# Hybrid decoder trunk on one core: stick weights as scan differences, value products in fours, narrow scores, and broadcast products moved ahead

## The chip, the cores and the metric

The kernel runs on one core of a Trainium2 chip. The metric is the device time of one execution in microseconds; the time before is the median of three runs. The engines are named as in the profile: PE is TensorE (its weight loads, which overlap its products, are PEld), DVE is VectorE, ACT is ScalarE, POOL is GpSimd, SP issues the DMAs. Matrix products write PSUM, which has eight banks here, and POOL works on SBUF alone.

## The reference, cut to what matters

Two layers. Each normalises the input, projects it once, mixes it with two kinds of attention, gates both and projects back.

```python
# A) stick-breaking attention, 4 heads x 64, strictly causal, blocks of 128
z = einsum(q, k) * scale
ls_z = log_sigmoid(z)
log_surv = where(mask, ls_z - z, 0)          # log(1 - sigmoid(z))
acc = (sum of log_surv over the later keys)
a = where(mask, exp(ls_z + acc), 0)          # sigmoid(z_k) * prod over later keys of (1 - sigmoid)
o = einsum(a, v)
# B) dilated sliding window, 12 heads x 64, patterns (128,1), (512,4), (2048,16)
s = where(mask, einsum(q, [k_prev, k_own]) * scale, -inf)
m = max(s); p = exp(s - m); l = sum(p); o = einsum(p, v) / l; log_den = m + log(l)
# over the three patterns
alpha = softmax(log_den); out = sum(alpha * o)
# each branch is gated, then one output projection, then the residual
```

S is 2048, the model width 1024. In pattern 0 as the kernel orders the keys, every block of 128 queries needs one block of 128 keys; in patterns 1 and 2 it needs its own block and the one before, except where the block is the first of its residue class.

## The kernel before, in words

A layer is a projection, the stick stage (`_stick`), the dilated stage (`_dilated`) and the output projection. The order of PE's instructions in both attention stages is held by hand (`pin`); on the other engines the framework orders the instructions.

**Stick stage.** Two head pairs. For each of the 16 blocks of queries, from the last to the first, the keys are taken from the diagonal back in pieces of up to 512: these are the units, 40 a pair, 80 a layer; 16 of a pair's 40 hold the diagonal and have one to four key blocks, the other 24 have four. `front(u)` makes the scores of both heads (lines 541 and 542, two products of the rounded float32 type; line 544 puts the mask on the diagonal). ACT makes `g`, the sigmoid of the negated score (line 549), and `b`, the sigmoid of the score (line 550). DVE's scan (line 551) multiplies `g` up from the last key to the first, and goes on in the next unit from the value that the previous unit left. POOL multiplies `b` by the scan (line 557). `mid(u)` transposes the weights on PE (line 570) and copies them to SBUF (line 572, head 0 on ACT, head 1 on DVE). `back(u)` multiplies them with the values (line 584). The loop issues `front(u + 2)`, `mid(u)`, and after every second unit `back` of the two units before. Buffers: six slices each for the scan, `g`, `b` and the transposed weights, four PSUM banks for scores, three for transposes.

**Dilated stage.** Six head pairs, 48 steps each: 16 blocks in each of the three patterns. `front(g)` makes the scores of both heads, two products per head with 256 key columns (line 732), also where only 128 are used; DVE adds the mask and takes the maximum (line 734), ACT makes the exponentials and their sum (line 738). `mid(g)` transposes (line 753) and copies (line 755, even steps on ACT, odd ones on DVE). Every fourth step `back` multiplies four steps with the values (line 767) and ACT copies the result (lines 772 to 777). Steps run three ahead. While a pair is under way, the statistics of the pair before are made (`stats_a` and `stats_b`, on POOL, PE, ACT and DVE, steps 1 and 5), and its three patterns are weighted: `weigh` broadcasts the weights by a product (line 837) and DVE multiplies (line 838), one call a step from step 15 to 30; `gate`, after every fourth of them, sums the patterns and gates them on POOL (lines 845 to 847). `make_q` orders the queries for patterns 1 and 2 by POOL copies (lines 668 and 672).

Of the kernel before, what the change touches and what calls it, by code (L numbers as in the profile page):

```python
# [13 lines left out]
AF = mybir.ActivationFunctionType  # L14
ALU = mybir.AluOpType
# [444 lines left out]
def _stick(tc, mem, sb_scr, g_scr, mix, ident, ident_r):  # L460
    nc = tc.nc
# [12 lines left out]
    setH = ("H5", "H4", "H3", "H2")  # L474
    wk0 = mem.get("G0", [128, 12, 513])
    wk1 = mem.get("G1", [128, 12, 512])
    r_s = Slices([wk0[:, i] for i in range(6)])
    gam = Slices([wk0[:, 6 + i] for i in range(6)])
    b_s = Slices([wk1[:, i] for i in range(6)])
    at_s = Slices([wk1[:, 6 + i] for i in range(6)])  # L480
    nc.gpsimd.memset(wk0[:, 6:12, 512:513], 1.0)
    qs_, ks1, ks2, vn, gt = {}, {}, {}, {}, {}

    def prep(pr, jq):
# [44 lines left out]
    pin = tc.keep_in_program_order  # L529
    carry, prod, ats, obs = {}, {}, {}, {}  # L530

    def front(u):
        pr, i, lo, hi = units[u]
        n, kq, top = hi - lo, lo // 512, hi == 128 * (i + 1)
        nn = max(n, 256)
        qs = slice(128 * (i % 4), 128 * (i % 4) + 128)
        zs = []
        for h in range(2):
            z = z_r.get([128, 512])
            qt = qs_[pr, i // 4, h][:, qs]  # L540
            pin(nc.tensor.matmul(z[:, :nn], qt, ks1[pr, kq, h][:, :nn], start=True, stop=False))
            pin(nc.tensor.matmul(z[:, :nn], qt, ks2[pr, kq, h][:, :nn], start=False, stop=not top))  # L542
            if top:
                pin(nc.tensor.matmul(z[:, n - 128:n], id_b, tri, start=False, stop=True))
            zs.append(z)
        prod[u] = []
        for h, z in enumerate(zs):
            b, g, r = b_s.get(), gam.get(), r_s.get()
            nc.scalar.activation(g[:, 512 - n:512], z[:, :n], AF.Sigmoid, scale=-0.125)  # L549
            nc.scalar.activation(b[:, :n], z[:, :n], AF.Sigmoid, scale=0.125)  # L550
            nc.vector.tensor_tensor_scan(  # L551
                out=r[:, 0:n + 1][:, ::-1], data0=g[:, 512 - n:513][:, ::-1],
                data1=z[:, 0:1].to_broadcast([128, n + 1]),
                initial=1.0 if top else carry[h][:, 0:1],
                op0=ALU.mult, op1=ALU.bypass)
            carry[h] = r
            nc.gpsimd.tensor_tensor(out=b[:, :n], in0=b[:, :n], in1=r[:, 1:n + 1], op=ALU.mult)  # L557
            prod[u].append(b)
        if pr == 0 and i % 4 == 0 and lo == 0:
            todo.append(prep(1, i // 4))  # L560
            next(todo[-1])

    def mid(u):
        pr, i, lo, hi = units[u]
        n = hi - lo
        ats[u] = []
        for h, b in enumerate(prod.pop(u)):
            ps = t_r.get([128, 512])
            for j in range(n // 128):
                pin(nc.tensor.transpose(ps[:, 128 * j:128 * j + 128], b[:, 128 * j:128 * j + 128], ident))  # L570
            at = at_s.get()
            (nc.vector.tensor_copy if h else nc.scalar.copy)(at[:, :n], ps[:, :n])
            ats[u].append(at)

    def back(u):
# [16 lines left out]
                nc.sync.dma_start(out=mix[0][pr].rearrange("p (c a) -> p c a", c=NT), in_=gt[pr])  # L592

    todo = []
    LEAD, BATCH = 2, 2
    load(1)
    for u in range(LEAD):
        front(u)
# [18 lines left out]
def _dilated(tc, mem, v_scr, qk_scr, g_scr, mix, masks, sel, ident, neg1):  # L617
    nc = tc.nc
    pin = tc.keep_in_program_order
    mk = mem.get("M", [128, 732])  # L620
# [3 lines left out]
    o_r = mem.bank_ring(5)  # L624
    w_r = mem.bank_ring(6, 7)
    pa, pb = mem.get("H0", [128, 2, 2, 256]), mem.get("H1", [128, 2, 2, 256])
    pe_s = Slices([pa[:, 0], pa[:, 1], pb[:, 0], pb[:, 1]])
    ta, tb = mem.get("H6", [128, 2, 2, 2, 128]), mem.get("H7", [128, 1024])
    td = mem.get("H5", [128, 2, 2, 2, 128])
    ts_s = Slices([td[:, 0], td[:, 1], ta[:, 0], ta[:, 1], tb[:, 0:512].rearrange("p (c h q) -> p c h q", c=2, h=2)])  # L630
    xa = mem.get("X", [128, 1024])
# [21 lines left out]
    def load_q(pr):  # L653
        qq[pr] = [[], []]
        for h in range(2):
            t = q_r.get([128, S])
            nc.sync.dma_start(out=t, in_=qk_scr[pr, h])
            qq[pr][h].append(t)
# [33 lines left out]
    for i in range(4):  # L692
        t = gt_r.get([128, 4, 128])
# [5 lines left out]
    def geom(p, b):  # L699
        if p == 0:  # L700
            return b, 0, True
        c, n = (b // 4, b % 4) if p == 1 else (0, b)
        return c, n, n == 0

    def front(g):
        pr, p, b = g // 48, g // 16 % 3, g % 16
        if (p, b) == (0, 0):
            o3s[pr] = mem.get(f"G{pr % 2}", [128, 3, NT, 128])
            sts[pr] = st_r.get([128, 2, 3, 2, NT])
        st = sts[pr]  # L710
        c, n, first = geom(p, b)
        u0 = 0
        if p == 0:
            w0 = min(b, 14) * 128
            u0 = 128 * b - w0
        else:
            run, stp = (32, 4) if p == 1 else (8, 1)
            w0 = 0 if first else run * (n - 1)
        un = 128 if first else 256
        m0 = M_OWN[p] + 128 - un  # L720
        sc = s_r.get([128, 2, 256])
        pe = pe_s.get()
        for h in range(2):
            qb = qq[pr][h][p].bitcast(F32R)[:, 128 * b:128 * b + 128]
            for s in range(2):
                kt = kk[pr][h][s]
                if p == 0:
                    kv = kt[:, w0:w0 + 256]
                else:
                    kv = kt.rearrange("p (c a) -> p c a", c=NT)[  # L730
                        :, c::stp, w0:w0 + 2 * run].rearrange("p c (w a) -> p w c a", w=2)
                pin(nc.tensor.matmul(sc[:, h], qb, kv, start=s == 0, stop=s == 1))  # L732
        for h in range(2):
            nc.vector.tensor_tensor_reduce(  # L734
                out=pe[:, h, :un], in0=sc[:, h, u0:u0 + un], in1=mk[:, m0:m0 + un],
                scale=-0.125, scalar=3.0e38, op0=ALU.add, op1=ALU.min,
                accum_out=st[:, 0, p, h, b:b + 1])
            nc.scalar.activation(pe[:, h, :un], pe[:, h, :un], AF.Exp, scale=-1.0,  # L738
                                 bias=st[:, 0, p, h, b:b + 1], accum_out=st[:, 1, p, h, b:b + 1])
        pes[g] = pe  # L740
# [3 lines left out]
    def mid(g):  # L744
        p, b = g // 16 % 3, g % 16
        first = geom(p, b)[2]
        pe = pes.pop(g)
        tp = t_r.get([128, 2, 2, 128])
        nch = 1 if first else 2
        for ch in range(nch):  # L750
            for h in range(2):
                w = 0 if first else 1 - ch
                pin(nc.tensor.transpose(tp[:, ch, h], pe[:, h, 128 * w:128 * w + 128], ident))  # L753
        ts = ts_s.get()
        (nc.vector.tensor_copy if g % 2 else nc.scalar.copy)(ts[:, :nch], tp[:, :nch])  # L755
        tss[g] = ts

    def back(g0):
# [37 lines left out]
    def stats_b(pr, eng):  # L796
# [3 lines left out]
        for s in range(2):  # L800
            ps = w_r.get([128, 512])
# [4 lines left out]
            for h in range(2):  # L806
                pin(nc.tensor.matmul(ps[:32, 256:384], mk[:, 656 - 16 * h:688 - 16 * h],
                                     x1[:, s, NT * h:NT * h + NT].rearrange("p j a -> p (j a)"),
                                     start=h == 0, stop=h == 1))
            nc.scalar.copy(sm[:, s].rearrange("p q a -> p (q a)"), ps[:32, :384])  # L810
        nm = sm[:, 0]
        ll = sm[:, 1]
        mn = tb[0:32, 896:1024]
        ew = tb[0:32, 512:896].rearrange("p (q a) -> p q a", q=3)
        nc.vector.tensor_tensor(out=mn, in0=nm[:, 0], in1=nm[:, 1], op=ALU.min)
        nc.vector.tensor_tensor(out=mn, in0=mn, in1=nm[:, 2], op=ALU.min)
        eng.tensor_tensor(out=ew, in0=mn.unsqueeze(1).to_broadcast([32, 3, 128]), in1=nm, op=ALU.subtract)
# [12 lines left out]
    def weigh(pr, c):  # L830
        o3 = o3s[pr]
        if c % 4 == 0:
            gts[pr] = gt_r.get([128, 4, 128])
            nc.sync.dma_start(out=gts[pr], in_=g_scr[2 + pr, :, 128 * c:128 * c + 512].rearrange(
                "p (c a) -> p c a", c=4))
        wb = w_r.get([128, 3, 128])
        pin(nc.tensor.matmul(wb, selr[:, c], wr, start=True, stop=True))
        nc.vector.tensor_tensor(out=o3[:, :, c], in0=o3[:, :, c], in1=wb, op=ALU.mult)
# [16 lines left out]
    LEAD = 3  # L855
# [3 lines left out]
    for g in range(total):  # L859
        pr, t = g // 48, g % 48  # L860
        if t % 8 == 2:
            load_v(g // 8 + 1)
        if t == 2:
            make_q(pr, 2)
        if pr + 1 < NPAIR:
            if t == 16:
                load_k(pr + 1)
            if t == 24:
                load_q(pr + 1)
            if t == 36:  # L870
                make_q(pr + 1, 1)
        if g + LEAD < total:
            front(g + LEAD)
        mid(g)
        if g % 4 == 0 and g:
            back(g - 4)
        if pr:
            if t == 1:
                stats_a(pr - 1, nc.gpsimd)
            elif t == 5:  # L880
                stats_b(pr - 1, nc.gpsimd)
            elif 15 <= t < 31:
                weigh(pr - 1, t - 15)
                if t % 4 == 2:
                    gate(pr - 1, (t - 15) // 4)
        yield
    back(total - 4)
    m7 = [mem.get("F5", [128, NT, 128], F32R), mem.get("F6", [128, NT, 128], F32R)]
# [93 lines left out]
```

## Time and profile before

| | |
|---|---|
| time, median of 3 runs | 3229.11 us (3222.7 to 3229.73) |
| profiled execution, its own time | 3228.57 us |
| its span, first to last instruction | 3226.8 us |
| mean granted TensorE clock | 0.993 |
| PE busy | 3137.9 us, 97% of the span |
| DVE busy | 1648.3 us, 51% |
| ACT busy | 1534.4 us, 48% |
| POOL busy | 1234.4 us, 38% |

The busy times are those of the whole span. Matmuls are pipelined and their ends are modelled, so PE's busy time contains short waits. Instructions of ACT and DVE are recorded with their latency: neighbours overlap by some tens of ns, and the distance from start to start is shorter than the duration. The chain of waits is followed back from the last instruction, at each step to what released it; a piece of it is the part of an instruction that the chain uses.

### The profile page before, as it was taken

The page shows a single profiled execution, that of the slowest core. Times are in us where ns is not written, and L with a number is a line of the kernel's source. Part 1 is how long each engine was busy: PE and PEld are TensorE (multiplying, and loading weights), DVE is VectorE, ACT ScalarE, POOL GpSimd, SP SyncE. Part 2 cuts the span into 40 slices and gives each one's busy share as a digit, 9 for nine tenths or more (in the row PEclk, how much of TensorE's full clock was granted, in tenths as well). Part 3 has the DMA queues.
Part 4 walks back from the last instruction along what each step waited for, and adds up shares of the span by engine and source line. Part 5 has one row for each costly group of instructions (what it writes and reads, how often), then busy time and mean ns, then how long its engine had stood idle before and what let it go on. Part 6 is the DMA issues. An engine that isn't in the chain of part 4 may idle for free.

```text
span 3226.8 us, 59494 instructions
## 1 busy us (share of the span) xinstructions
PE 3137.9 (97%) x21968; PEld 2683.2 (83%) x21968; DVE 1648.3 (51%) x4147; ACT 1534.4 (48%) x4317; POOL 1234.4 (38%) x1302
## 2 busy tenths in 40 slices
PE   8999999999999999989999999999999999999899
PEld 8888888887777999878898888888877789988787
DVE  6134440015988777764141444301169887777721
ACT  5123331114878998962031233211158789988510
POOL 1067751102664444451010677511036734444500
PEclk9999999999999999999999999999999999999999
DMA  5123346317023556454442233463160235663443
GB/s 198 63 73 113 112 138 181 122 48 204 15 83 93 165 155 193 117 164 150 128 135 72 70 113 105 149 189 104 59 186 21 83 106 151 178 187 100 140 145 108
DMA packets 324066, 396.40 MB, mean 123 GB/s; under 512 B 20160, under 2 KB 270016, under 8 KB 313536
## 3 DMA queue, kind: packets, MB, share of 16 engines
q1 hardware_dynamic: 323776, 392.60, 40.0%
q8 instruction: 174, 2.85, 0.4%
q14 instruction: 116, 0.95, 0.1%
HBM read 235.24 MB, written 148.90 MB: 119 GB/s over the span
## 4 chain that ended last, share of the span: by engine, by line
PE 81%; DVE 5%; ACT 4%; POOL 4%; issue 3%; DMA 2%; SPq 0%; POOLq 0%; ACTq 0%; DVEq 0%
PE b L310 11%; PE b L311 11%; PE b L309 11%; PE b L732 7%; PE b L767 5%; PE b L753 5%; PE b L451 4%; PE b L453 4%; PE b L452 4%; PE b L935 4%; PE b L936 4%; PE b L932 3%; PE b L584 3%; PE b L367 2%; ACT H L738 2%
## 5 line engine op out<-in xcount | busy, mean ns | idle before, releaser
L738 ACT ACTIVATE H<-H,T 128x256 f32<-128x256 f32 (+1 forms) x1152 | 522.7, 457 | 45.9 <-DVE T L734 43.4
L311 PE MATMUL b<-F,F 128*128 128x512 f32 (+1 forms) x1344 | 484.1, 360 | 0.4 <-DVE F L282 0.3
L734 DVE CUSTOM_DVE_ANT_0 H<-b,M 128x256 f32<-128x256 f32 (+1 forms) x1152 | 368.6, 361 | 168.9 <-PE b L732 66.2
L732 PE MATMUL b<-F,F 128*128 128x256 f32 x2304 | 412.3, 303 | 0.3 <-DVE T L734 0.3
L557 POOL TENSOR_TENSOR G<-G,G 128x512 f32<-128x512 f32 (+3 forms) x320 | 320.5, 1017 | 228.5 <-DVE G L551 171.6
L551 DVE TENSOR_TENSOR_SCAN G<-G,b 128x513 f32<-128x513 f32 (+3 forms) x320 | 336.5, 1085 | 33.0 <-ACT G L550 32.7
L732 PEld LDWEIGHTS b<-F,F 128*128 128x128 f32 x2304 | 326.4, 190 | 20.1 <-issue 19.5
L310 PE MATMUL b<-F,G 128*128 128x512 f32 (+1 forms) x896 | 324.7, 362 | 0.0
L309 PE MATMUL b<-F,G 128*128 128x512 f32 (+1 forms) x896 | 324.3, 362 | 0.0
L310 PE MATMUL b<-F,F 128*128 128x512 f32 (+1 forms) x896 | 323.2, 361 | 0.0
L309 PE MATMUL b<-F,F 128*128 128x512 f32 (+1 forms) x896 | 321.9, 359 | 0.0
L753 PE MATMUL b<-ident,H 128*128 128x128 f32 x1800 | 292.9, 274 | 11.4 <-ACT H L755 5.5
L311 PEld LDWEIGHTS b<-F,F 128*128 128x128 f32 x1344 | 253.7, 189 | 38.4 <-DVE F L282 0.8
L135 POOL TENSOR_SCALAR U<-U 128x16 f32<-128x16 f32 (+1 forms) x80 | 33.7, 421 | 536.1 <-DVE U L334 315.5
L767 PE MATMUL b<-H,H 128*64 128x128 f32 x3600 | 229.8, 277 | 0.8 <-DVE H L755 0.8
L753 PEld LDWEIGHTS b<-ident,H 128*128 128x128 f32 x1800 | 215.6, 141 | 16.5 <-ACT H L755 8.6
L549 ACT ACTIVATE G<-b 128x512 f32<-128x512 f32 (+3 forms) x320 | 179.5, 563 | 103.6 <-PE b L542 87.8
L738 ACT ACTIVATION_READ_ACCUMULATOR H<-H,T 128x1 f32 x1152 | 219.3, 190 | 0.0
L767 PEld LDWEIGHTS b<-H,H 128*64 128x64 f32 x3600 | 193.8, 137 | 25.9 <-issue 23.4
L212 POOL TENSOR_TENSOR F<-H,F 128x1024 fp32r<-128x1024 f32 x22 | 53.9, 2456 | 380.7 <-ACT F L211 164.0
L333 ACT ACTIVATE H<-b 128x512 f32<-128x512 f32 x96 | 57.5, 600 | 294.8 <-PE b L311 293.8
L309 PEld LDWEIGHTS b<-F,G 128*128 128x128 f32 x896 | 168.9, 189 | 26.6
(165 smaller groups left out, 6844.2 us busy)
## 6 DMA issues: line engine op xcount, KB each, us to landing
qk_l<-H SPq DMA_DIRECT2D x192, 256.0 KB
F<-qk_l SPq DMA_DIRECT2D x48, 1024.0 KB
v_l<-S SPq DMA_DIRECT2D x288, 128.0 KB
H<-v_l SPq DMA_DIRECT2D x72, 512.0 KB
F<-qk_l SPq DMA_DIRECT2D x48, 512.0 KB
g_l<-S SPq DMA_DIRECT2D x64, 256.0 KB
G<-mixa_l SPq DMA_DIRECT2D x32, 448.0 KB
H<-in_w_in SPq DMA_DIRECT2D x24, 512.0 KB
```

The lines of the kernel that those rows point to most:

```text
L309: nc.tensor.matmul(ps, hT(q, 0, k)[:, cs], wh, start=k == 0, stop=False)
L310: nc.tensor.matmul(ps, hT(q, 0, k)[:, cs], wl, start=False, stop=False)
L311: nc.tensor.matmul(ps, hT(q, 1, k)[:, cs], wh, start=False, stop=k == NK - 1)
L451: nc.tensor.matmul(ps, wh[:, k, w], hT(tq, 0, k), start=k == 0, stop=False)
L549: nc.scalar.activation(g[:, 512 - n:512], z[:, :n], AF.Sigmoid, scale=-0.125)
L551: nc.vector.tensor_tensor_scan(out=r[:, 0:n + 1][:, ::-1], data0=g[:, 512 - n:513][:, ::-1], data1=z[:, 0:1].to_broadcast([128, n + 1]), i ...
L557: nc.gpsimd.tensor_tensor(out=b[:, :n], in0=b[:, :n], in1=r[:, 1:n + 1], op=ALU.mult)
L732: pin(nc.tensor.matmul(sc[:, h], qb, kv, start=s == 0, stop=s == 1))
L734: nc.vector.tensor_tensor_reduce(out=pe[:, h, :un], in0=sc[:, h, u0:u0 + un], in1=mk[:, m0:m0 + un], scale=-0.125, scalar=3.0e38, op0=ALU. ...
L738: nc.scalar.activation(pe[:, h, :un], pe[:, h, :un], AF.Exp, scale=-1.0, bias=st[:, 0, p, h, b:b + 1], accum_out=st[:, 1, p, h, b:b + 1])
L753: pin(nc.tensor.transpose(tp[:, ch, h], pe[:, h, 128 * w:128 * w + 128], ident))
L767: pin(nc.tensor.matmul(ob[64 * h:64 * h + 64, b % 4], vq[(pr * 3 + p) * 2 + (b - ch) // 8][:, (b - ch) % 8, 64 * h:64 * h + 64], ts[:, ch, h],
```

## The change

In the stick stage a weight is written as the difference of two neighbouring values of the scan, `r[k+1] - r[k]`, in place of sigmoid times scan; the second sigmoid goes, all copies of transposed weights go to ACT, value products are issued for four units at a time, the scan and `g` have four slices, the transposed weights ten. In the dilated stage a step that uses one key block makes scores of 128 columns; the copies of the transposed exponentials go to ACT in one step of four and to DVE in three; the exponentials have a fifth buffer, for which the statistics move to other places; `weigh` and `gate` run from step 17 to 32 and stand between `front` and `mid` of their step.

```diff
-    r_s = Slices([wk0[:, i] for i in range(6)])
-    gam = Slices([wk0[:, 6 + i] for i in range(6)])
+    r_s = Slices([wk0[:, i] for i in range(4)])
+    gam = Slices([wk0[:, 4 + i] for i in range(4)])
     b_s = Slices([wk1[:, i] for i in range(6)])
-    at_s = Slices([wk1[:, 6 + i] for i in range(6)])
-    nc.gpsimd.memset(wk0[:, 6:12, 512:513], 1.0)
+    at_s = Slices([wk1[:, 6 + i] for i in range(6)] + [wk0[:, 8 + i, :512] for i in range(4)])
+    nc.gpsimd.memset(wk0[:, 4:8, 512:513], 1.0)
...
             nc.scalar.activation(g[:, 512 - n:512], z[:, :n], AF.Sigmoid, scale=-0.125)
-            nc.scalar.activation(b[:, :n], z[:, :n], AF.Sigmoid, scale=0.125)
...
-            nc.gpsimd.tensor_tensor(out=b[:, :n], in0=b[:, :n], in1=r[:, 1:n + 1], op=ALU.mult)
+            nc.gpsimd.tensor_tensor(out=b[:, :n], in0=r[:, 1:n + 1], in1=r[:, 0:n], op=ALU.subtract)
...
-            (nc.vector.tensor_copy if h else nc.scalar.copy)(at[:, :n], ps[:, :n])
+            nc.scalar.copy(at[:, :n], ps[:, :n])
...
-    LEAD, BATCH = 2, 2
+    LEAD, BATCH = 2, 4
...
-    pe_s = Slices([pa[:, 0], pa[:, 1], pb[:, 0], pb[:, 1]])
     ta, tb = mem.get("H6", [128, 2, 2, 2, 128]), mem.get("H7", [128, 1024])
+    pe_s = Slices([pa[:, 0], pa[:, 1], pb[:, 0], pb[:, 1], tb[:, 512:1024].rearrange("p (h k) -> p h k", h=2)])
...
-        u0 = 0
-        if p == 0:
-            w0 = min(b, 14) * 128
-            u0 = 128 * b - w0
-        else:
+        un = 128 if first else 256
+        if p:
             run, stp = (32, 4) if p == 1 else (8, 1)
             w0 = 0 if first else run * (n - 1)
-        un = 128 if first else 256
...
-                    kv = kt[:, w0:w0 + 256]
+                    kv = kt[:, 128 * b:128 * b + 128]
...
-                        :, c::stp, w0:w0 + 2 * run].rearrange("p c (w a) -> p w c a", w=2)
-                pin(nc.tensor.matmul(sc[:, h], qb, kv, start=s == 0, stop=s == 1))
+                        :, c::stp, w0:w0 + run * un // 128].rearrange("p c (w a) -> p w c a", a=run)
+                pin(nc.tensor.matmul(sc[:, h, :un], qb, kv, start=s == 0, stop=s == 1))
...
-                out=pe[:, h, :un], in0=sc[:, h, u0:u0 + un], in1=mk[:, m0:m0 + un],
+                out=pe[:, h, :un], in0=sc[:, h, :un], in1=mk[:, m0:m0 + un],
...
-        (nc.vector.tensor_copy if g % 2 else nc.scalar.copy)(ts[:, :nch], tp[:, :nch])
+        (nc.scalar.copy if g % 4 == 1 else nc.vector.tensor_copy)(ts[:, :nch], tp[:, :nch])
...
-        mn = tb[0:32, 896:1024]
-        ew = tb[0:32, 512:896].rearrange("p (q a) -> p q a", q=3)
+        mn = xa[0:32, 768:896]
+        ew = nm
...
             front(g + LEAD)
+        if pr and 17 <= t < 33:
+            weigh(pr - 1, t - 17)
+            if t % 4 == 0:
+                gate(pr - 1, (t - 17) // 4)
         mid(g)
...
-            elif 15 <= t < 31:
-                weigh(pr - 1, t - 15)
-                if t % 4 == 2:
-                    gate(pr - 1, (t - 15) // 4)
```

## Rows read from the trace of the kernel before

**Rows 1.** Busy us by stretch: length, PE, PEld, DVE, ACT, POOL (instructions), clock, DMA.
```profile
765.00:1016.00 251.00, 231.67 (x2115) 186.35 (x2114) 224.76 (x272) 185.00 (x416) 164.75 (x168) 0.98 0.28 80
1016.00:1400.00 384.00, 376.23 (x3866) 345.99 (x3867) 286.06 (x1355) 349.68 (x1336) 163.96 (x209) 1.00 0.54 153
1104.94:1123.07 18.13, 18.13 (x188) 17.11 (x189) 17.16 (x69) 16.04 (x58) 13.65 (x17) 1.00 0.46 139
2365.00:2620.00 255.00, 236.00 (x2141) 189.93 (x2139) 225.88 (x272) 186.17 (x417) 164.73 (x168) 0.98 0.29 84
```

**Rows 2.** Groups by form, 765 to 1016: busy us, mean ns, idle before.
```profile
L551 DVE TENSOR_TENSOR_SCAN G<-G,b 128x513 f32<-128x513 f32 x112 | 138.5, 1263 | 16.5 <-ACT G L550 16.5
L557 POOL TENSOR_TENSOR G<-G,G 128x512 f32<-128x512 f32 x112 | 129.4, 1163 | 106.1 <-DVE G L551 78.8 <-PE b L570 22.4 <-PE b L542 3.0
...
L550 ACT ACTIVATE G<-b 128x512 f32<-128x512 f32 x112 | 70.0, 628 | 0.0
...
L572 DVE COPY G<-b 128x512 f32<-128x512 f32 x56 | 37.5, 670 | 1.9 <-PE b L570 1.6
```

**Rows 3.** Chain of waits, 984 to 1002: start us, us, what.
```profile
984.81 1.90 PE b L584 x32
986.71 0.43 PE b L541
987.14 0.24 PE b L542
...
987.89 0.42 ACT G L550
...
989.33 0.62 ACT G L572
...
990.61 1.90 PE b L584 x32
```

**Rows 4.** Timeline, 990 to 997: start us, us, instruction, idle before and releaser.
```profile
993.20 0.60 ACT L549 ACTIVATE G<-b 128x512 f32<-128x512 f32 x1 [1.77 <-PE b L542]
...
994.32 1.28 DVE L551 TENSOR_TENSOR_SCAN G<-G,b 128x513 f32<-128x513 f32 x1 [0.59 <-ACT G L550]
...
995.75 1.28 POOL L557 TENSOR_TENSOR G<-G,G 128x512 f32<-128x512 f32 x1 [1.20 <-DVE G L551]
```

**Rows 5.** Chain of waits, 1024 to 1036 (pattern 0, first pair).
```profile
1026.33 1.55 ACT H L738 x8
1027.88 0.26 ACT H L755
...
1028.92 0.47 ACT G L772
...
1030.43 1.55 ACT H L738 x8
```

**Rows 6.** Chain of waits, 1146 to 1174 (pattern 0, third pair).
```profile
1151.00 1.02 PE b L767 x16
...
1157.13 1.02 PE b L767 x16
...
1159.05 0.47 PE b L732 x4
...
1160.74 2.29 POOL F L672 x4
...
1166.21 0.44 PE b L837
...
1167.35 1.03 PE b L767 x16
```

**Rows 7.** Groups by form, whole span: DVE copy of a narrow step.
```profile
L755 DVE COPY H<-b 128x256 f32<-128x256 f32 x96 | 40.2, 418 | 0.0
```

**Rows 8.** Pieces of the chain: rounded transposes, and float32 products of 128 columns.
```profile
214.23 1.32 PE b L367 x16
...
1153.39 0.44 PE b L807 x4
```

## The prediction

> **What bounds the kernel now.** I read the views in this order: busy time by stage, the groups of the stick-breaking stage, the chain of waits inside a few of its cycles, and then the chain in the dilated stage. Only these two stages are touched, and the second layer repeats the first.
>
> Busy time by stage [rows 1] shows TensorE (PE) busy for 231.67 of the 251 us of the stick stage, and for 376.23 of the 384 us of the dilated stage. PE therefore nearly sets the pace of both. Time can be won only from its idle remainder, 19.3 us in each stick stage (19.0 in the second layer) and 7.8 us in a dilated stage, or from PE's own work. PE's ends are modelled, so short waits hide in its busy time and the remainder is a lower bound.
>
> In the stick stage VectorE (DVE) is nearly as full, 224.76 us. Its scans take 1263 ns, its copies 670 [rows 2]. The chain over one cycle of two full units [rows 3] runs from one burst of value products at 984.81 to the next at 990.61, that is 5.80 us. The burst takes 1.90, two score products 0.67, then four sigmoids on ScalarE (ACT), one behind the other from 987.4 to 989.3 (one of their pieces is shown), then the ACT copy of 0.62 that the next transposes wait for. The second sigmoid thus stands in the chain, and the scan waits for it too: in the timeline [rows 4] the first sigmoid starts at 993.20, the scan only at 994.32, 0.59 us idle, released by L550. GpSimd (POOL) starts its product 0.15 us after the scan's end.
>
> In the dilated stage, pattern 0 of a layer's first head pair is a chain of ACT alone [rows 5]: 4.10 us for a group of four steps (1026.33 to 1030.43), made of eight exponentials at 0.39 (1.55 for four), two copies of 0.26 and one of 0.47. In later pairs the chain is PE's [rows 6]: per group one burst of 1.02, scores at 0.47 a step and transposes, about 4.0. There the group with the statistics takes 6.13 (1151.00 to 1157.13), and the next two take 10.22 (to 1167.35). Two plain groups and the first broadcast product (0.44) would be 8.5, so 1.7 us are the wait of that product for POOL, whose work in the chain starts with a cast at 1160.74 and lets the product go at 1166.21. Three weighting groups in pattern 1 [rows 1] last 18.13 us, with PE busy without a gap and DVE for 17.16 us.
>
> **The change part by part: the stick stage.** The sum is made against the profiled execution, 3228.57 us (its span is 3226.8); the median of the runs shown is 3229.11, half a microsecond more.
>
> *Second sigmoid out, difference instead of product.* 160 ACT instructions a layer of at most 628 ns [rows 2] go. The POOL instruction stays one subtraction for one product, with the same sizes; I price it the same, 1.16 us, bounds zero either way since no engine or operand size changes. What comes out of the chain is two sigmoids per unit, about 1 us per unit, in a loop that PE closes anyway.
>
> *All copies to ACT.* 80 copies a layer leave DVE (the 56 full ones are 37.5 us [rows 2], the 24 shorter about 0.4 each), and ACT takes them at 0.62 or less [rows 3]. ACT loses 0.63 and gains 0.62 on one of its two heads: it ends with two sigmoids fewer and one copy more per unit. DVE falls from 224.76 by some 47 to 178 us and is no longer beside PE.
>
> *Value products of four units.* The work is the same. Half of the restarts fall away: the first score product after a burst takes 0.43 where the second takes 0.24 [rows 3], so about 0.2 us for 20 bursts a layer, 4 us. But the burst grows to 2 x 1.90 = 3.8 us, and nothing else can be issued on PE behind it. Scores are issued two units ahead, so the scans of two units must cover it. Worked through for four full units: burst 3.8, first scores 0.67, one sigmoid 0.6, two units of scans 4 x 1.26 = 5.0, subtraction 1.2, last transposes 0.4: 11.7 us, against 2 x 5.80 = 11.6 now. Full units win nothing. But 16 of the 40 units of a head pair have one to four blocks at the diagonal, mean 2.5, so a unit has 3.4 blocks in the mean. There the loop shrinks with the blocks to some 10.0 us, while the stage now takes 251 us for 20 such sets, 12.5 each with the start. The ceiling is PE's idle time and the restarts, 19 + 4 = 23 us a layer; the floor of the gain is none. I take 15, two thirds of the ceiling: **-30 us** for both layers.
>
> *Fewer scan and gate buffers (six to four).* A scan must wait for the subtraction two units back instead of three. Two units are four scans of 1.26 us, and the subtraction ends 1.4 us after its scan [rows 4], so it is covered; uncovered it would cost up to 1.2 us per unit where POOL is held up. Nothing.
>
> **The dilated stage.** *128 keys instead of 256.* 21 of the 48 steps of a pair (16 in pattern 0, four in pattern 1, one in pattern 2) with four products each, 12 pairs: 1008 products. Today one takes 0.47 / 4 = 0.119 us [rows 6]. The trace has no such product with 128 columns. Below, the nearest row is the 128-column transposes of the same rounded type, each with its own weights, 1.32 / 16 = 0.082 [rows 8]. Above, it is a plain float32 product of 128 columns, two instructions of 0.44 / 4 = 0.11 each, 0.22 [rows 8]. I take 0.082, because type and weight load are the same. In pattern 0 this frees PE (by 0.6 us per group), and ACT sets the pace. In the other first steps it frees 0.15 us each; of five a pair I count the two that lie outside weighting groups: 0.3 x 12, with the first pairs of the layers -4.5 us.
>
> The Trainium skill, "TensorE: Matmul & The Clock Gate", section "LDWEIGHTS (loading the stationary operand)", prices a load of 128 columns at 107 ns whatever the product. By it a narrow product would save 12 ns, not 37, the last term would be -1.4, and the forecast 3 us higher. The transposes of [rows 8], at 0.082 with their loads, disagree.
>
> *Copies of the exponentials, ACT from one half to one quarter.* A pattern-0 group loses one of its two 0.26 copies on ACT: 4.10 becomes 3.84. Later pairs, at 4.0, gain less; I take 0.21 x 4 groups x 12 pairs = **-10 us**. DVE gets one copy more per group. Outside the weighting it has room. In it, three groups use 17.16 of 18.13; three copies of 418 ns [rows 7] bring 18.4. DVE then sets these groups: 6.13 against 6.04, a loss of at most 0.3 x 10 = 3 us by recorded durations, which overlap a little. I count nothing, and no gain for the first steps there.
>
> *Weighting two steps later and ahead of the transposes.* The broadcast product waits for POOL by 1.7 us in the pair shown; PE's whole idle time gives 7.8 / 5 = 1.6 a pair. Two steps are 2 us or more, less the 0.8 that pattern 0 is now quicker. I take 1.0 of it in ten pairs: **-10 us** (bounds 0 and -15.6). The gate loads and stores move with it on SP's queue and nothing waits for them closely; the three GpSimd gate instructions move by two steps. Ahead of the transposes the product now fills the time in which PE waits for exponentials, and its multiplication stands on DVE ahead of the copy, which delays that copy by some 0.55 us; four steps of lead cover it.
>
> *Fifth exponential buffer, statistics in place:* they take waits away that the chain does not show. Nothing.
>
> Sum: -30 - 10 - 10 - 4.5 = -54.5, so 3228.57 - 54.5 = **3174 us**.
>
> **The rivals.**
> 1. *The long burst holds the stick stage.* Speaking for it: the loop of 11.7 against 11.6 above. Against it: the small units. The stick gain falls to about 4 us; 3228.6 - 4 - 24.5 = 3200 us.
> 2. *The narrow product is dear, the kernel slower.* If a rounded product of 128 columns costs the 0.22 of the float32 one, a pattern-0 group needs 3.98 + 16 x 0.101 = 5.6 us of PE instead of 4.05: 1.55 x 48 = +74. The other first steps add 20 x 0.101 x 12 = +24. The two terms of -10 (copies) and -4.5 are gone: 3228.6 + 98 - 30 - 10 = 3287 us. It decides from the price where 1008 products eat the 40 us of the rest, 0.16 us each. For it speaks that no narrow product of this type is in the trace; against it, that the transposes of that type and width run at 0.082.
> 3. *The stick stage reaches PE's floor:* 23 us a layer, 3228.6 - 46 - 24.5 = 3158 us. For it: DVE and ACT both fall far below PE. Against: PE's order is fixed and each unit passes three other engines in turn.
> 4. *The change only moves waits:* DVE sets the weighting groups, the stick copies queue behind sigmoids, the stall at the broadcast stays with POOL. The rest is little more than ACT's 10 us and some of the stick's; 3220 us, up to no difference.
>
> **How the numbers follow.** Forecast 0.46 (its own range 3160 to 3190), rival 1 0.17, rival 2 0.17, rival 3 0.12, rival 4 0.08. The time is the likeliest's, 3174. The range takes in the forecast and rivals 1 and 3 and part of 4, and leaves out rival 2: 3140 to 3225. Within 0.2% (6.5 us, about what a measurement of this kernel tells from no change) lies most of rival 4 alone, 0.07. Slower is rival 2 less its near end, 0.16. Faster is the rest, 0.77.
>
> **What would show it.** The stick stages last some 236 and 240 us; DVE's share falls to 75%; PE's idle time there halves; bursts of up to 64 value products stand about 11 us apart. In the dilated stage the narrow products start 0.08 to 0.09 us apart, a pattern-0 group takes 3.8, and the wait at the first broadcast is gone. Narrow products 0.2 us apart, scans idle for more than 1.5 us after each burst, or weighting groups over 6.2 us with DVE full would prove it wrong, by rival 2, 1 or 4.

## The result, and the profile after

| | before | after |
|---|---|---|
| median | 3226.94 us (3222.7 to 3229.73) | 3197.75 us (3195.6 to 3198.26) |
| profiled execution, its own time | 3228.57 us | 3197.81 us |
| span | 3226.8 us | 3195.4 us |

The ratio is 0.9909 [0.9892, 0.9927]: faster by 0.9%, inside the range, but 24 us behind the forecast of 3174. Between the two profiled spans 31.4 us are gone. I cut each layer at the first score product of the stick stage, its last value product, and the first and last output product. The stick stages went from 250.6 and 250.2 us to 235.9 and 238.9 (-26.0), the dilated stages from 406.1 and 409.2 to 401.8 and 401.5 (-12.0), and the output stages from 197.1 and 193.2 to 200.3 and 195.6, so they took 5.6 more. The rest of the kernel took about 1 us more. The first is near its forecast (-30), the second is half of its own (-24.5), and the third was not foreseen.

Busy time of the changed kernel by stretch; columns as in [rows 1].

```profile
765.20:1001.20 236.00, 221.74 (x2113) 183.47 (x2111) 183.39 (x191) 154.86 (x336) 150.26 (x168) 0.99 0.29 85
1001.20:1394.00 392.80, 386.85 (x3983) 349.43 (x3979) 324.28 (x1460) 337.00 (x1296) 171.05 (x217) 1.00 0.55 158
```

In the first stick stage PE's idle time fell by 5.1 us, from 19.3 to 14.3, and did not halve; the other 10 us came out of PE's *busy* time (231.67 to 221.74), which as recorded contains short waits and restarts. DVE fell by 41 us to 78% of the stage. In the dilated stage DVE rose to 324 us.

The same kernel's groups by form, over both layers; columns as in [rows 2].

```profile
L550 DVE TENSOR_TENSOR_SCAN G<-G,b 128x513 f32<-128x513 f32 x224 | 269.4, 1256 | 73.6 <-ACT G L549 63.8 <-issue 8.3 <-POOL G L556 1.0
L556 POOL TENSOR_TENSOR G<-G 128x512 f32<-128x512 f32 x224 | 234.6, 1049 | 213.1 <-DVE G L550 171.2 <-PE b L569 13.1 <-PE b L544 10.4
L571 ACT COPY G<-b 128x512 f32<-128x512 f32 x224 | 126.0, 607 | 12.8 <-PE b L569 11.5
L727 PE MATMUL b<-F,F 128*128 128x128 f32 x1008 | 163.5, 286 | 2.3 <-DVE T L729 2.3
```

The second sigmoid is gone (it was L550; that line is now the scan), all copies are ACT's, and there are 1008 narrow score products, as counted. The chain of waits over two sets of four units in the stick stage, to be read against [rows 3]:

```profile
958.93 3.21 PE b L583 x56
962.14 0.43 PE b L541
...
962.84 0.61 ACT G L549
...
963.53 0.44 DVE G L550
...
966.04 0.50 PE b L541
...
970.04 3.00 PE b L583 x52
...
979.90 3.44 PE b L583 x60
```

Bursts of 52 to 60 value products stand 11.1 and 9.9 us apart. Behind the first, PE is out of the chain from 962.82 to 966.04: a sigmoid, then scans, before the next unit's scores. Behind the second it is out as long, from 973.71 to 976.94. The waits of this stage (line waited for, us in total, times, longest) count it:

```profile
ACT G L549 <- PE b L542: 51.6, 18, 6.5
DVE G L550 <- ACT G L549: 32.5, 18, 3.4
```

The scans stand idle 18 times, 1.8 us in the mean. That is the sign that the prediction named for rival 1. What this wait costs is read under e3.

The chain in pattern 0 of the first head pair, against [rows 5]:

```profile
1010.05 3.09 ACT H L733 x16
1013.15 0.47 ACT G L767
1013.62 0.27 ACT H L750
1013.88 3.09 ACT H L733 x16
```

In this stretch ACT alone sets a group of four steps, with one copy of 0.27 in it: 3.83 us, forecast 3.84. The gain is smaller than the forecast all the same. From one burst of value products to the next, the four groups took 3.99, 3.99, 4.01 and 4.95 us before the change and take 3.83, 3.83, 4.15 and 4.98 now, so 0.15 us is won over the four, where the term of the copies counted 0.84.

A later head pair of the changed kernel, in stretches: its three weighting groups, then the four groups ahead of them.

```profile
1087.99:1106.69 18.70, 18.70 (x187) 16.78 (x186) 18.17 (x72) 14.81 (x55) 12.35 (x15) 1.00 0.50 160
1067.88:1087.99 20.11, 19.80 (x198) 16.99 (x197) 15.02 (x80) 18.04 (x77) 8.09 (x12) 1.00 0.87 225
```

The four groups ahead of them in the same pair of the kernel before:

```profile
1083.99:1104.87 20.88, 20.45 (x198) 17.69 (x198) 14.71 (x78) 19.36 (x82) 8.49 (x13) 1.00 0.82 232
```

They took 20.88 us there, so 0.77 is won. This pair won least: over the eight pairs that are neither first nor last of their layer, the four groups fell from 21.46 to 20.08 us in the mean, by 1.4. The three weighting groups took 18.13 [rows 1], so 0.57 is lost, and now DVE is busy for 18.17 of 18.70. The timeline inside one of them shows what PE waits for:

```profile
1094.17 1.94 PE L762 MATMUL b<-H,H 128*64 128x128 f32 x28
...
1094.25 0.55 DVE L833 TENSOR_TENSOR G<-G,b 128x384 f32<-128x384 f32 x1
...
1094.72 0.68 DVE L750 COPY H<-b 128x512 f32<-128x512 f32 x1
...
1095.45 0.42 PEld L762 LDWEIGHTS b<-H,H 128*64 128x64 f32 x8 [0.21 <-DVE H L750]
```

The burst of value products (L762) has begun, and its last weights wait 0.21 us for a copy (L750) that stands on DVE behind the multiplication of the broadcast (L833).

### The profile page after: what moved, and what is told of

The parts are those of the page before. It is cut to its first block, busy times and chain, and to the rows that moved or that the text cites. A ratio compares the mean times of both kernels' runs of the same rounds, so it can differ in the third digit from the quotient of the medians.

```text
span 3195.4 us, 59386 instructions
## 1 busy us (share of the span) xinstructions
PE 3121.5 (98%) x21968; PEld 2668.3 (84%) x21968; DVE 1629.7 (51%) x4131; ACT 1428.3 (45%) x4013; POOL 1207.4 (38%) x1302
## 4 chain that ended last, share of the span: by engine, by line
PE 88%; DVE 4%; DMA 2%; ACT 2%; POOL 2%; issue 2%; SPq 0%; DVEq 0%; POOLq 0%; ACTq 0%
PE b L310 11%; PE b L311 11%; PE b L309 11%; PE b L727 7%; PE b L762 6%; PE b L748 5%; PE b L583 4%; PE b L451 4%; PE b L453 4%; PE b L452 4%; PE b L930 4%; PE b L931 4%; PE b L927 4%; PE b L569 3%; PE b L367 2%; PE b L541 2%
## 5 line engine op out<-in xcount | busy, mean ns | idle before, releaser
L729 DVE CUSTOM_DVE_ANT_0 H<-b,M 128x256 f32<-128x256 f32 (+1 forms) x1152 | 371.1, 360 | 111.6 <-PE b L748 42.1
L727 PE MATMUL b<-F,F 128*128 128x256 f32 (+1 forms) x2304 | 408.2, 301 | 2.3 <-DVE T L729 2.3
L556 POOL TENSOR_TENSOR G<-G 128x512 f32<-128x512 f32 (+3 forms) x320 | 291.9, 924 | 233.1 <-DVE G L550 191.1
L550 DVE TENSOR_TENSOR_SCAN G<-G,b 128x513 f32<-128x513 f32 (+3 forms) x320 | 326.0, 1079 | 75.1 <-ACT G L549 65.1
L727 PEld LDWEIGHTS b<-F,F 128*128 128x128 f32 x2304 | 312.2, 191 | 31.4 <-issue 26.5
L311 PEld LDWEIGHTS b<-F,F 128*128 128x128 f32 x1344 | 253.7, 189 | 37.7 <-DVE F L282 0.3
L750 DVE COPY H<-b 128x512 f32<-128x512 f32 (+1 forms) x432 | 241.5, 559 | 1.0 <-PE b L748 0.7
L762 PE MATMUL b<-H,H 128*64 128x128 f32 x3600 | 237.2, 279 | 0.0
L762 PEld LDWEIGHTS b<-H,H 128*64 128x64 f32 x3600 | 194.6, 137 | 31.7 <-issue 22.5
L549 ACT ACTIVATE G<-b 128x512 f32<-128x512 f32 (+3 forms) x320 | 163.0, 557 | 124.6 <-PE b L542 107.5
L927 PE MATMUL b<-F,H 128*128 128x512 f32 x448 | 180.6, 403 | 12.3 <-ACT F L911 12.3
```

Source lines behind the costliest of these rows:

```text
L311: nc.tensor.matmul(ps, hT(q, 1, k)[:, cs], wh, start=False, stop=k == NK - 1)
L550: nc.vector.tensor_tensor_scan(out=r[:, 0:n + 1][:, ::-1], data0=g[:, 512 - n:513][:, ::-1], data1=z[:, 0:1].to_broadcast([128, n + 1]), i ...
L556: nc.gpsimd.tensor_tensor(out=b[:, :n], in0=r[:, 1:n + 1], in1=r[:, 0:n], op=ALU.subtract)
L727: pin(nc.tensor.matmul(sc[:, h, :un], qb, kv, start=s == 0, stop=s == 1))
L729: nc.vector.tensor_tensor_reduce(out=pe[:, h, :un], in0=sc[:, h, :un], in1=mk[:, m0:m0 + un], scale=-0.125, scalar=3.0e38, op0=ALU.add, op ...
L750: (nc.scalar.copy if g % 4 == 1 else nc.vector.tensor_copy)(ts[:, :nch], tp[:, :nch])
```

## The experiments

Each time below is a median, except that of e8, which is one execution. Each ratio is to runs of the kernel before on the same chip. The experiments ran on three chips, on which the kernel before took 3224.98 (e9, e10) to 3227.59 us (e5 to e8), so where two experiments are compared, the difference of their gains over the kernel before is given too. Stage lengths come from one profiled execution each. e11 and e12 turned out to be one program run twice (below): their medians differ by 0.6 us, but their stages by up to 2.9 us. Stage differences of 3 us are therefore read as scatter unless a chain shows the cause.

**e1 and e2: one part alone.** e1 is the kernel before with the new `_stick`, e2 with the new `_dilated`.

> The stick part alone, the dilated stage as before. If the changed kernel's stage times add up, the two stick stages fall by 14.5 and 11.4 us as they do there, nothing else moves: 3227 - 26 = 3201 us. If the stick gain only exists because the later stage takes the place of what waits, this run gives less: 3210 or more.

> The dilated part alone. By the changed kernel's trace the dilated stages win 4.3 and 7.5 us and the output stages behind them lose 3.5 and 2.5: 3227 - 6 = 3221 us. By the prediction's own terms (copies -10, stall -10, narrow scores -4.5) it would be 3203 us.

e1: 3202.89 us, ratio 0.9931 [0.9915, 0.9946], 23.5 us won. e2: 3223.63 us, ratio 0.9989 [0.998, 0.9999]; the dilated stages were 4.5 and 7.9 us shorter, the output stages 2.6 and 3.5 longer. So the stick part is the gain. The dilated part is nearly nothing in the net, and it is this part that lengthens the output stages.

**e3: value products in twos.**

```diff
-    LEAD, BATCH = 2, 4
+    LEAD, BATCH = 2, 2
```

> The changed kernel with value products issued for two units at a time again (buffers stay at ten). If the long burst starves the scans, twos win 4 to 6 us a layer: about 3188 us. If PE's own work sets the stick stage, only the restarts come back, 20 a layer at 0.2 us: about 3206 us.

3194.98 us, 0.9902 [0.9888, 0.9917]; the interval overlaps that of the change. The stick stages were 236.3 and 234.4 us, so the time fits neither theory. But the stage holds two effects that nearly cancel. Between the two head pairs of a stage PE waits for the keys of the second pair (L542), whose last load is L510. The changed kernel issues it ahead of a load for the dilated stage (L648):

```profile
891.68 0.59 SPq L510 DMA_DIRECT2D H<-F  x1
892.36 0.57 SPq L648 DMA_DIRECT2D F<-qk_l  x1
...
895.59 0.76 PE L542 MATMUL b<-H,F 128*128 128x512 f32 x1 [4.00 <-DMA H<-F]
```

In e3 the load for the dilated stage comes first:

```profile
890.35 0.46 SPq L648 DMA_DIRECT2D F<-qk_l  x1
...
892.61 0.57 SPq L510 DMA_DIRECT2D H<-F  x1
...
900.10 0.77 PE L542 MATMUL b<-H,F 128*128 128x512 f32 x1 [9.79 <-DMA H<-F]
```

PE waits 9.79 us instead of 4.00, and 9.7 to 10.1 us in the second layer of e3 and in both layers of e11 and e12, which have the twos and this order too. Without this one wait, the six stick stages with twos last 224.2 to 228.1 us, and six with fours (those of the change, e1 and e9) 231.9 to 234.9. So the long burst does hold the stage, by some 7 us a layer, and the later arrival of the keys takes most of that back. PE's wait for the scans, before it can load the next scores, bears it out; the changed kernel's, then that of e3:

```profile
PEld b L541 <- DVE G L550: 8.4, 20, 0.7
```

```profile
PEld b L541 <- DVE G L550: 2.1, 12, 0.2
```

The scans' own idle time is no measure of it: in e3 it is 32.1 us in 29 waits, against 32.5 in 18. That the order of the loads is what lengthens the wait for the keys is argued; twos with the keys loaded first were not run.

**e5 and e8: the price of a narrow product.** e5 gives the narrow steps back their 256 key columns, 128 of which are not used; e8 cuts each product of pattern 0 into two of 64 columns.

```diff
# e5
-                    kv = kt[:, 128 * b:128 * b + 128]
+                    kv = kt[:, 128 * min(b, 14):128 * min(b, 14) + 256]
...
# e8
...
+                    for lo in (0, 64):
+                        pin(nc.tensor.matmul(sc[:, h, lo:lo + 64], qb, k0[:, lo:lo + 64], start=True, stop=False))
+                        pin(nc.tensor.matmul(sc[:, h, lo:lo + 64], qb, kv[:, lo:lo + 64], start=False, stop=True))
```

> The changed kernel with 256-column scores in every step again. If the narrow products, which measured 0.112 us from start to start in place of 0.119, still matter because a pattern-0 group is PE's as well as ACT's, pattern 0 goes back to 4.0 us a group and the kernel to some 3206 us. If ACT alone sets pattern 0, as the prediction has it, nothing moves: 3198 us.

> The changed kernel with each 128-column score product of pattern 0 cut into two of 64 columns: the same columns, twice the products and weight loads. If the 0.112 us of a narrow product is the floor set by its weight load, each half costs that as well, pattern-0 groups go to 5.4 us and the kernel up by some 75 us. If it is a rate per column, halves start 0.056 us apart and the time stays within 10 us.

e5: 3204.14 us, 0.9927 [0.9912, 0.9941], 6.4 us more than the change (5.7 by the gains); its dilated stages are 4.5 and 4.0 us longer. So the narrow products do earn something, though the intervals overlap. The chain of e5, then of the changed kernel, each in pattern 0 of the second pair, four score products a piece:

```profile
1074.68 0.47 PE b L728 x4
```

```profile
1072.58 0.40 PE b L727 x4
```

So a narrow product takes 0.10 in the chain, a wide one 0.12. In the first pair the chain of e5 is PE's alone:

```profile
1008.67 1.02 PE b L763 x16
...
1012.66 1.02 PE b L763 x16
```

That is 3.99 us a group, as before the change, though ACT has only one copy left in it. So ACT sets the 3.83 us of the changed kernel only because the scores are narrow as well.

e8: 3316.07 us. Its chain of waits, at half clock in the first pair and at full clock in a later one:

```profile
1008.74 0.21 PE b L729
1008.95 0.21 PE b L728
...
1099.94 0.11 PE b L729
1100.05 0.11 PE b L728
```

At full clock 64 columns take 0.11, no less than 128. Up to 128 columns the price is one for each product and not for each column. The Trainium skill, "TensorE: Matmul & The Clock Gate", section "LDWEIGHTS (loading the stationary operand)", puts a load of weights at its columns divided by 1.2, in ns, so 107 for 128 columns, an estimate by that formula. The 0.11 of these products agrees with it; the transposes of [rows 8], at 0.082 each with a load of its own, do not, and no run separates the load from the product. e8's time says less, since the clock fell too (last section).

**e6 and e10: who copies the exponentials.** e6 shares the copies evenly, as before the change; e10 only in steps 17 to 32 of the pairs that weight.

```diff
# e6
-        (nc.scalar.copy if g % 4 == 1 else nc.vector.tensor_copy)(ts[:, :nch], tp[:, :nch])
+        (nc.vector.tensor_copy if g % 2 else nc.scalar.copy)(ts[:, :nch], tp[:, :nch])
# e10
+        t = g % 48
+        even = g >= 48 and 17 <= t < 33
+        (nc.scalar.copy if (g % 2 == 0 if even else g % 4 == 1) else nc.vector.tensor_copy)(ts[:, :nch], tp[:, :nch])
```

> The changed kernel with the copies of transposed exponentials half on ACT and half on DVE again. The prediction's -10 us for pattern 0 come back (4.1 us a group), and if the copies on DVE are what stretches the weighting groups to 6.19 us, those fall to 6.0 and give 6 us: about 3201 us, with the two seen apart in the groups. If the weighting groups stay at 6.19, 3208 us.

> The changed kernel with the copies of the exponentials shared evenly by VectorE and ScalarE in steps 17 to 32 of the pairs that weight, and one in four on VectorE elsewhere reversed as changed. If VectorE's queue stretches the weighting groups (18.00 of 18.50 us busy) and the copies are what can be taken from or given to it, the groups come to 6.0 us from 6.2 while the first four groups of a pair stay as changed: 3192 to 3194 us. Rival: the place of the broadcast in VectorE's queue sets them; then the groups stay at 6.2 us and the time is 3197 to 3199 us.

e6: 3195.29 us, 0.9903 [0.9886, 0.9919]: the copies on DVE earn nothing. e10: 3195.84 us, 0.9913 [0.9898, 0.9927]. Its stretches of the same pair, weighting groups first:

```profile
1088.49:1106.59 18.10, 18.10 (x187) 16.82 (x186) 16.60 (x66) 15.55 (x58) 12.33 (x15) 1.00 0.49 157
1067.97:1088.49 20.52, 19.98 (x197) 16.94 (x197) 15.62 (x83) 18.40 (x79) 8.07 (x12) 1.00 0.90 232
```

With DVE down to 16.60 the weighting groups are back at 18.10: DVE's queue did stretch them. But the group just ahead of them grew from 5.35 to 5.77 us, so this pair wins 0.2 us, and in some pairs the second group grew as well (4.66 to 5.65). The expected time was not reached.

**e4, e7 and e9: when and where the weighting stands.** e7 keeps its place ahead of the transposes and goes back to steps 15 to 30; e4 undoes both; e9 undoes both in the last pair alone.

```diff
# e7 (e4: the same calls behind mid(g))
-        if pr and 17 <= t < 33:
-            weigh(pr - 1, t - 17)
+        if pr and 15 <= t < 31:
+            weigh(pr - 1, t - 15)
...
# e9
-        if pr and 17 <= t < 33:
+        if 0 < pr < NPAIR - 1 and 17 <= t < 33:
...
+            elif pr == NPAIR - 1 and 15 <= t < 31:
+                weigh(pr - 1, t - 15)
...
```

> The changed kernel with weighting and gating in steps 15 to 30 behind the transposes, as before the change. If the new place costs (weighting groups 6.19 instead of 6.03 us, and the last gate two steps later holds up the output weights), the kernel gets faster, to 3190 us. If it pays as predicted (the wait at the first broadcast, 10 us for both layers), it gets slower, to 3206 us.

> The changed kernel with weighting in steps 15 to 30 but still ahead of the transposes: only the time of the move is undone, not its place. If the place ahead of the transposes delays DVE's copies, the weighting groups stay at 6.19 us and the time near 3197. If the two later steps are what costs, it is as with both undone: 3193 us.

> The changed kernel, in which the last head pair alone weights in steps 15 to 30, behind the transposes, as before; the other pairs are as changed. If the late last gate is what is given back (page G0 comes free late, the loads of w_out queue behind the last gate's store, and the last pair's third weighting group takes 9.8 us), that group and the output stages return to before's (about 198 and 193 us) and the time is 3192 to 3194 us. Rival: the place of the weighting ahead of the transposes costs in every pair alike; then the last pair holds an eighth of that and the time is 3197 to 3198 us.

e7: 3195.78 us, 0.9904 [0.9889, 0.9919]. The four groups ahead of the weighting in the same pair:

```profile
1068.39:1089.61 21.22, 20.19 (x200) 17.36 (x199) 16.00 (x82) 18.25 (x77) 9.02 (x13) 1.00 0.85 238
```

They take 21.22 us against 20.11: the stall at the first broadcast is back, 1.1 us a pair, as its chain shows:

```profile
1079.01 2.23 POOL F L671 x4
...
1082.83 0.44 PE b L832
```

Yet the time is no longer than that of the change. The stall's 11 us are made good at the end of the layers: output stages of 198.5 and 191.3 us against 200.3 and 195.6, and a third weighting group of 6.7 us in the last pair of each layer against 9.8 and 9.3. e4: 3192.82 us, 0.9895 [0.9879, 0.9912]. Its stretches of the same pair:

```profile
1090.69:1108.54 17.85, 17.85 (x186) 16.83 (x185) 17.79 (x70) 14.72 (x54) 13.57 (x17) 1.00 0.43 149
1069.85:1090.69 20.84, 20.04 (x199) 17.25 (x198) 15.90 (x82) 18.11 (x76) 8.28 (x13) 1.00 0.94 247
```

Against e7 (18.53 and 21.22) only the place differs: behind the transposes both stretches are shorter, 1.1 us a pair, with DVE as busy (17.79 against 18.00). The dilated stages bear it out (401.5 and 399.0 us, against 404.9 and 405.6). The medians differ by 3.0 us only, since the stick stages, whose code is the same, were 2.7 and 2.8 us longer in e4's profile, and the second output stage 3.0. So the place ahead of the transposes is a cost by itself, some 10 us by the stages. The time does not establish it: 3.0 us by the medians, 1.7 by the gains, with overlapping runs.

e9: 3188.65 us, 0.9889 [0.9873, 0.9906], 9.1 us under the change (7.1 by the gains), more than expected. The other pairs take 66.4 us as in the change; the last one, between its first and last burst, falls from 65.4 and 65.3 to 62.4 and 63.1, and the output stages to 198.5 and 193.9. The chain of the changed kernel in that pair's third weighting group:

```profile
1368.70 2.46 DVE X L786 x3
1371.16 0.20 DVE H L729
...
1371.58 0.92 DVE X L786
1372.50 0.46 DVE G L833
```

And of e9 in its place:

```profile
1369.23 1.39 DVE X L786 x2
1370.63 0.46 DVE G L833
1371.09 0.17 DVE X L786
...
1372.15 0.18 DVE X L786
```

L786 is the beginning of the last pair's own statistics, which in this pair run on DVE. Its four instructions need the sums of pattern 1, which ends with step 31. In the change the weighting is then still under way on a full DVE, and they stand 3.38 us in the chain ahead of the masks (L729), copies (L750) and multiplications of the broadcast (L833) of the steps; in e9, where the weighting is two steps further on, 1.74 us. The last pair explains 5.2 us (3.0 and 2.2), the output stages 3.5.

**e11 and e12: the best of these together.** e11 is e9 with BATCH = 2; e12 issues the combination of the statistics in four steps.

> The changed kernel with its value products in twos (as e3) and the last pair's weighting two steps earlier, behind the transposes (as e9). If the two are independent, the 2.8 us of the one and the 9.1 us of the other add: 3185 to 3187 us. If the twos' gain lay in the dilated stage's start or in the last pair's schedule, which e9 has already mended, 3188 to 3190 us.

> As e11, and the combination of the statistics in the later pairs is issued in four steps (5 to 8) where it all stood in step 5, so that VectorE's mask-and-maximum of the next steps no longer stands behind the minimum and the reciprocal (which wait 1.23 us for ScalarE and 1.21 us for GpSimd in the changed kernel). If these waits are what makes the second group of a later pair 4.7 us where the first pair's takes 3.83, that group comes to 3.9 to 4.2 us in ten pairs, and the time is 5 to 8 us under e11, 3178 to 3181 us. Rival: the first broadcast then waits for the later weights, or the third group takes the wait: the time is that of e11 within 2 us.

e11: 3189.05 us, 0.988 [0.9866, 0.9895], the same as e9 within the scatter. As issued here, the twos add nothing that the time shows; their wait for the second pair's keys is 9.7 and 9.9 us here too. e12: 3189.67 us, 0.9882 [0.9865, 0.9898]. It tested nothing: the framework orders DVE, ACT and POOL itself and put the instructions of all engines into the order of e11. What it gives is the repeat.

## Why the prediction was right in sign and too hopeful in size

- *Stick, -30:* right in size, and in part by luck. The profile shows -26.0, e1 alone -23.5. But the 15 us a layer were taken as two thirds of a ceiling and not worked out. Rival 1's wait exists (18 waits of 1.8 us) and the long burst costs some 7 us a layer, so the rival had a mechanism that is there; but it left 4 us of the stick gain, and the rest of the stick part outweighed it. In e3, e11 and e12 a burst half as long ends the stage hardly earlier, because another wait grew from 4.0 to 9.8 us. Rival 3 fell, 14.3 us of idle PE remain. No run separates the second sigmoid from the copies.
- *Copies, -10:* this step failed, in two places. The gain was too large: in the first pair a group does come to 3.83 us, but it had taken 3.99 from burst to burst and not the 4.10 of the piece of ACT's chain, since PE's own work took as long (e5), and the third group gave back nearly half of what the first two won. In a later pair the four groups won 1.4 us in the mean, and e7 puts 1.1 of it down to the stall. Then "I count nothing" for DVE in the weighting groups: 0.57 us a pair came back there, nearly twice the 0.3 that I had bounded, with the place of the broadcast as a second cause (e10 and e4 each bring these groups down). Rival 4 named this wait, and was right for this part; its sign, groups over 6.2 us with DVE full, is there (6.23 in the mean). e6 puts the net of the copies at nothing.
- *Weighting later, -10:* right as to the stall, 1.1 us a pair in e7 against 1.0. What failed is "nothing waits for them closely". In the last pair the later weighting meets the statistics on DVE, and the output stage takes longer; e9 gets 7 to 9 us back by undoing the change there. With both moves undone everywhere (e4) the kernel is 4 to 5 us faster than with them, so in the net this term earned nothing. The part "four steps of lead cover it" for the copy behind the multiplication failed too: the timeline shows the burst waiting for that copy.
- *Narrow products, -4.5:* e5 puts it at -6.4 (-5.7 by the gains), nearly right for a wrong reason, and so by luck. The price is 0.10 to 0.11, not 0.082, so one saves about half of the 0.037 counted or less; the transposes of [rows 8] were no measure for it. But more of them count than I had let count. "ACT sets the pace" in pattern 0 held only with narrow scores: with wide ones PE holds a group at 3.99 us (e5). By the Trainium skill's load of 107 ns (the section named at e8), all 1008 would give 12 us, an estimate with every one of them on PE's path. Rival 2's 0.22 fell.

So the missing 24 us are 4 of the stick part, about 10 of the copies, and 7 to 9 of the last pair and the output stages, less the 1 to 2 that the narrow products gave beyond their term; the rest, some 2 to 5 us, is within the scatter of the stages. This account adds differences of single runs, and parts of it share causes. How the output stage comes to lose the 1.8 and 1.7 us that e9 gives back is argued only: the gates end later, and the loads for the output stage are queued behind the last gate's store on SP (first at 1382.15 us in the change, 1378.62 in e9). The other 2.1 of its 5.6 us stay open. Weighting two steps later but behind the transposes, in all pairs but the last, was not tried.

## What to carry to other kernels

Work that moves later to escape a stall has to be followed to its last repetition: there it met work of the next stage, and most of the gain was given back at a place that none of the middle repetitions shows. An engine with room over a stage may have none in one group of it, so a copy should be priced group by group. Where a framework orders an engine's queue, look at the order that came out before reading a time as a test. And where an experiment changes nothing in the time, look for a second wait that grew: the shorter bursts won 7 us a layer and lost 6 at one load.

## What was not expected of the hardware

Products of 64 columns brought the granted clock down. In e8, by stretch:

```profile
1003.00:1008.00 5.00, 5.00 (x49) 4.83 (x46) 3.40 (x18) 3.28 (x15) 0.00 (x0) 1.00 0.73 147
1008.00:1014.00 6.00, 6.00 (x33) 6.00 (x32) 2.21 (x14) 3.12 (x15) 0.00 (x0) 0.52 0.56 231
...
1090.00:1100.00 10.00, 10.00 (x105) 8.93 (x105) 5.21 (x33) 7.48 (x31) 0.99 (x1) 1.00 1.03 271
```

PE is recorded as busy without a gap from 1003 on, largely by these products, and from 1008 the clock is at its lower level of 1.2 GHz and a product takes 0.21 instead of the 0.11 that it takes in the later pair, around the end of the last stretch shown. The change's products of 128 columns ran at 1.00 in the same place. The other surprise is GpSimd's instruction, which the prediction had priced the same: a subtraction of two neighbours of one buffer took 1049 ns where the product of two buffers took 1163 [rows 2], with the same columns. Whether the operation, the operands or DVE's lower load did it stays open.
